# Causal attention in a two-layer trunk: the mask moves from 64 TensorE products into a custom VectorE operation, and the first scores from double to single PSUM banks

## The chip, the cores and the metric

The kernel runs on one core of a Trainium2 chip. The metric is the device time of one execution in microseconds (us); less is better. The time before is the median of three runs.

## The reference, cut to what matters

All of it is float32, with a batch of 1, a sequence of 1024 and a model width of 1024. There are two layers: an mLSTM mixer with an MLP, then causal latent attention (8 heads) with an MLP. The change touches the causal softmax of the second layer:

```python
def block(args):                     # 128 queries of all heads
    qn_b, qr_b, start = args
    s = (jnp.einsum('bqhd,bkhd->bhqk', qn_b, k_nope)
         + jnp.einsum('bqhd,bkd->bhqk', qr_b, k_rope)).astype(jnp.float32) * scale
    qpos = start + jnp.arange(B_QBLOCK, dtype=jnp.int32)
    s = jnp.where(kpos[None, :] <= qpos[:, None], s, -jnp.inf)
    p = jax.nn.softmax(s, axis=-1)
    return jnp.einsum('bhqk,bkhd->bqhd', p.astype(v.dtype), v)
```

Around it, each layer computes `x + g1 * rmsnorm(mixer(modulate(rmsnorm(x))))` and then `x + g2 * rmsnorm(mlp(modulate(rmsnorm(x))))`, and the modulation (`ada`) comes from products of a condition vector with wide weight matrices.

## The kernel before, in words

Products of float32 tensors are made of three products of parts: each factor is split into a high and a low part, and `mm3` (L255, L256, L257) adds low x high, high x low and high x high in one PSUM bank. Weights come by DMA into `raw`, a ring of four 128x1024 buffers in SBUF; ScalarE copies out the high part (L190, L549) and VectorE subtracts it for the low part (L191, L550). The rows of probabilities, `pr`, lie in the same ring.

PSUM has eight banks of 128 x 512 floats: `ps` and `pc` are rings of two single banks, `pm` is a ring of two double banks. The dense stream of the MLPs accumulates in `pm` and `ps`; VectorE takes the sums out of `pm` at L199. `pc` serves transposes and small projections.

`two_streams` weaves two generators: the dense stream of an MLP, and the other one, which has the attention. The sequence is done in two halves of 512 queries. While the attention of the first half runs (955 to 1210 us), the dense stream is layer 0's MLP for the second half; while that of the second half runs (1565 to 1825 us), it is the MLP of layer 1 for the first. A scheduler then orders each engine's queue from its own estimates of how long instructions take; a kernel's queues are worked off in that order.

The attention works in units: one head and a pair of blocks of 128 queries, j = 0 and 1 in the first half, j = 2 and 3 in the second. The two blocks of a unit, e = 0 and 1, see n = (2j + e + 1) x 128 keys. A unit goes like this:

- `score_mm` makes the scores of one block, per group of up to 512 keys (at least 256 columns wide): four products at L1584 to L1587, for the group that holds the diagonal the mask product at L1589, and the last product at L1590. The mask product adds `maskA` (0 on and below the diagonal, -1e30 above) to 128 columns, with the bf16 identity `identb`. There are 64 of them. L1586 and L1587 need T, the turned rope part of the queries, which VectorE finishes at L1570.
- For j = 0 and 1 both blocks of a unit share one `pm` (a bank for each); for j = 2 and 3 each block has its own `pm`.
- `softmax` takes the negative maximum of the row (L1594, VectorE), scales it (L1595), makes the exponential of the scores with that as bias and with their sum (L1596, ScalarE, from PSUM into `pr`), inverts the sum (L1597) and normalises the row (L1598). POOL clears the 128 columns behind the shorter block's row (L1600).
- `attend` turns the probabilities by transposes into `pc` (L1704), splits them, and multiplies them with the values in `ps`.

At the start of the kernel SyncE's queue loads x, the first weights of the first projection (L1926) and the modulation weights of the first part (L376, L341); TensorE sums the modulation up (L344, L356), and the first dense products (L255) wait for the modulated x. The mask constants are built there too, on POOL and VectorE.

Of the kernel before, what the change touches and what calls it, by code (L numbers as in the profile page):

```python
# [11 lines left out]
BF16 = mybir.dt.bfloat16  # L12
I32 = mybir.dt.int32
AF = mybir.ActivationFunctionType
ALU = mybir.AluOpType
AX = mybir.AxisListType

P = 128
D = 1024
S = 1024  # L20
H = 512
# [62 lines left out]
def kernel(  # L84
# [27 lines left out]
    nc = tc.nc  # L112
# [4 lines left out]
    ts = lambda i, n: slice(i * n, (i + 1) * n)  # L117
# [18 lines left out]
    def tmp(dt=F32):  # L136
        return sb.tile([P, 512], dt, tag="tmp", bufs=TMP, name=f"tmp_{next(uid)}")

    def tmc(dt=F32):
        return sb.tile([P, 512], dt, tag="tmc", bufs=TMC, name=f"tmc_{next(uid)}")  # L140
# [10 lines left out]
    def pc():  # L151
        return pp.tile([P, 512], F32, tag="pc", bufs=2, name=f"pc_{next(uid)}")

    def pm():
        return pp.tile([P, 2, 512], F32, tag="pm", bufs=2, name=f"pm_{next(uid)}")

    def const(shape, dt, name):
        return sb.tile(shape, dt, tag=name, bufs=1, name=name)
# [102 lines left out]
    ident = const([P, P], F32, "ident")  # L261
# [186 lines left out]
    def gate(i, g, s):  # L448
        nc.vector.tensor_mul(mods[:, i], g, s)
        return mods[:, i]  # L450

    identb = const([P, P], BF16, "identb")
    nc.vector.tensor_copy(identb, ident)
    maskA = const([P, P], BF16, "maskA")
    mt = tmp()
    nc.gpsimd.memset(mt[:, :P], 0.0)
    nc.gpsimd.affine_select(
        out=mt[:, :P], in_=mt[:, :P], pattern=[[-1, P]], compare_op=ALU.is_ge,
        fill=-1e30, base=0, channel_multiplier=1,
    )  # L460
    nc.vector.tensor_copy(maskA, mt[:, :P])

    e8 = const([P, NH], F32R, "e8")
    nc.vector.memset(e8.bitcast(F32), 0.0)
# [15 lines left out]
    Cst = const([P, 4, VE], F32, "Cst")  # L480
# [39 lines left out]
    def sums_rstd(acc, n, y):  # L520
        pt = pc()
        nc.tensor.matmul(pt, ones, acc, start=True, stop=True)
        v, t = tmc(), acc
        nc.vector.tensor_scalar(v, pt, 1.0 / n, EPS, ALU.mult, ALU.add)
        rsqrt_(y, v, t)
        return y
# [838 lines left out]
    def rope_perm():  # L1365
        for q in range(4):
            nc.vector.tensor_copy(perm[:, ts(q, 32)], ident[:, ts(q ^ 1, 32)])
# [50 lines left out]
    def latent(hf, behind):  # L1418

        ready = []

        def load(b):
            with tc.high_priority(PRIO):
                w = []
                for i in range(2):
                    t = raw(F32R)
                    if i == 0:
                        t = sb.tile([P, 1024], F32R, tag="ws", bufs=WS, name=f"lw_{next(uid)}")  # L1430
                    nc.sync.dma_start(t.bitcast(F32), lw[b, i])
                    w.append(t.rearrange("p (a b) -> p a b", b=P))
                ready.append(w)

        load(0)
        load(1)
        yield 0
        h = hf.xn

        def proj(b):  # L1440
            if b < 4:
                load(b + 2)
            w, pt = ready.pop(0), pc() if b == 2 else ps()
            for k in range(KD):
                mm3(pt, w[0][:, k], w[1][:, k], h.hi[k], h.lo[k], k == 0, k == KD - 1)
            return pt

        lb = lambda b: lbias[:, b : b + 1]
        hf.cs = hdv()
        for i in range(2):  # L1450
            nc.sync.dma_start(hf.cs[:, i], rope_d[i][:, ts(hf.i, H)])
        if hf.i:
            hf.kk = [hd(F32R), hd(F32R)]
            for i in range(2):
                nc.sync.dma_start(hf.kk[i][:, 0:H].bitcast(F32), kkd[i])
        else:
            t = hdv(F32R)
            hf.kk = [t[:, 0], t[:, 1]]
        s = ts(hf.i, H)
        ck, cq0, cq1 = k4v(), k4v(), k4v()  # L1460
        cq = [cq0[:, 0], cq0[:, 1], cq1[:, 0]]
        def scaled(o, m):

            pt = proj(m)

            if not rx:
                rx.append(sums_rstd(hf.xx, D, Cst.rearrange("p a b -> p (a b)")[:, :H]))
            nc.vector.tensor_mul(o, pt, rx[0])
            return o

        def based(o, m):
            nc.scalar.activation(o, scaled(o, m), AF.Identity, bias=lb(m))

        rx = []
        for m in range(2):
            based(ck[:, m], m)
        rp = rope(scaled(tmc(), 2), hf, lb(2))
        next(rp)
        yield 0
        rs = rstd_steps([ck[:, 0], ck[:, 1]], 256)  # L1480
        next(rs)
        based(cq[0], 3)
        yield 0
        kr = last_of(rp)
        rstd_k = last_of(rs)
        nc.scalar.copy(hf.kk[0][:, s], kr)
        nc.vector.tensor_sub(hf.kk[1][:, s], kr, hf.kk[0][:, s].bitcast(F32))
        if not hf.i:
            for i in range(2):
                nc.sync.dma_start(kkd[i], hf.kk[i].bitcast(F32))  # L1490
        for m in range(1, 3):
            based(cq[m], 3 + m)
        yield 0
        behind()
        rs = rstd_steps(cq, 384)
        next(rs)
        hi, lo = k4v(F32R), k4v(F32R)
        with paced():
            for m in range(2):
                u = ck[:, m]  # L1500
                nc.vector.scalar_tensor_tensor(u, u, col(KVL + m, 1), rstd_k, ALU.mult, ALU.mult)
                split_mod(hi[:, m], lo[:, m], u, None)
        hf.ckv = ([hi[:, m] for m in range(2)], [lo[:, m] for m in range(2)])
        yield 3 - hf.i
        rstd = last_of(rs)
        yield 0
        ah, al, b = k4v(F32R), k4v(F32R), k4v(F32R)
        his, los = [ah[:, 0], ah[:, 1], b[:, 0]], [al[:, 0], al[:, 1], b[:, 1]]
        for m in range(3):
            u = cq[m]  # L1510
            nc.vector.scalar_tensor_tensor(u, u, col(QL + m, 1), rstd, ALU.mult, ALU.mult)
            split_mod(his[m], los[m], u, None)
        hf.cq = (his, los)
        yield 1

    SCALE = float((128 + 64) ** -0.5)
# [56 lines left out]
    def score_mm(o2, kk, q, kn, i):  # L1573

        qn, T = q
        qs = ts(i % 4, P)
        n = (i + 1) * P
        qh, ql, qT = qn[:, 0, qs], qn[:, 1, qs], T[:, qs]
        for g in range((n + 511) // 512):
            w = max(256, min(512, n - g * 512))  # L1580
            o = o2(g)
            ks = slice(g * 512, g * 512 + w)
            kh, kl = kn[0][:, ks], kn[1][:, ks]
            nc.tensor.matmul(o[:, :w], ql, kh, start=True, stop=False)  # L1584
            nc.tensor.matmul(o[:, :w], qh, kl, start=False, stop=False)
            nc.tensor.matmul(o[:, :w], qT, kk[1][:, ks], start=False, stop=False)  # L1586
            nc.tensor.matmul(o[:, :w], qT, kk[0][:, ks], start=False, stop=False)  # L1587
            if g == i // 4:
                nc.tensor.matmul(o[:, ts(i % 4, P)], identb, maskA, start=False, stop=False)  # L1589
            nc.tensor.matmul(o[:, :w], qh, kh, start=False, stop=True)  # L1590

    def softmax(f, pr, n, even):
        m, l = small(1), small(1)
        nc.vector.reduce_max(m, f, axis=AX.X, negate=True)  # L1594
        nc.vector.tensor_scalar(m, m, SCALE, None, ALU.mult)  # L1595
        nc.scalar.activation(pr[:, :n], f, AF.Exp, bias=m, scale=SCALE, accum_out=l)  # L1596
        nc.vector.reciprocal(l, l)  # L1597
        nc.vector.tensor_scalar(pr[:, :n], pr[:, :n], l, None, ALU.mult)  # L1598
        if even:
            nc.gpsimd.memset(pr[:, n : n + P], 0.0)  # L1600

    def scores(kk, unit):

        (_, q, kn, _), j = unit
        prs = []
        if j < 2:
            st = pm()
            pr = raw().rearrange("p (a b) -> p a b", b=512)
            for e in range(2):
                score_mm(lambda g: st[:, e], kk, q, kn, 2 * j + e)  # L1610
            for e in range(2):
                n = (2 * j + e + 1) * P
                softmax(st[:, e, :n], pr[:, e], n, e == 0)
                prs.append(pr[:, e])
        else:
            for e in range(2):
                st = pm()
                n = (2 * j + e + 1) * P
                score_mm(lambda g: st[:, g], kk, q, kn, 2 * j + e)
                pr = raw()  # L1620
                softmax(st.rearrange("p a b -> p (a b)")[:, :n], pr, n, e == 0)
                prs.append(pr)
        return prs
# [549 lines left out]
    drain(p1)  # L2173
    two_streams(with_weight_sums(f0), behind(bg_latent(), 4))
    rope_perm()


    B = {}
# [91 lines left out]
    fill = all_out()  # L2270
    v = None
    dense = mlp(1, hfs[1], u1, [4] * 8, True, B)
    n = 0
# [34 lines left out]
```

## Time and profile before

| | |
|---|---|
| median of 3 runs | 2361.49 us (2361.12 to 2361.56) |
| the profiled execution | 2359.22 us |
| its span | 2357.3 us |
| mean granted TensorE clock | 0.997 |
| TensorE, VectorE, ScalarE, POOL busy | 98%, 68%, 47%, 7% |
| first attention, 955 to 1210 us: TensorE, VectorE busy | 250.9, 194.7 us |
| second attention, 1565 to 1825 us: TensorE, VectorE busy | 255.2, 159.1 us |

A group's row gives line, engine, operation, output <- inputs, shape and count, then busy us and mean ns, then the idle time before it and what ended that. In a timeline the columns are start and duration in us, and a bracket holds the idle time ahead of the instruction and its releaser. Matmuls are pipelined: each is listed with its whole passage, so several overlap, and the room that one takes is read from start to start. PEld is the loading of weights for them.

### The profile page before, as it was taken

How to read it: one execution, taken by the hardware profiler on the slowest of the kernel's cores; microseconds unless marked ns; L12 is line 12 of the kernel's file. 1: busy time of each engine (PE TensorE's matmuls, PEld its weight loads, DVE VectorE, ACT ScalarE, POOL GpSimd, SP SyncE). 2: the span in 40 equal slices, each digit the busy share in tenths (PEclk: the TensorE clock that was granted, in tenths of full speed). 3: DMA queues.
4: the chain of work that ended last, by engine and by line, in shares of the span. 5: the costliest groups of instructions: out<-in, count | busy, mean ns of one | idle time of the engine just before them, and what ended most of it. 6: DMA issues, size and time to landing. Idle time of an engine off the chain costs nothing.

```text
span 2357.3 us, 32527 instructions
## 1 busy us (share of the span) xinstructions
PE 2321.8 (98%) x12181; PEld 1959.9 (83%) x12181; DVE 1605.7 (68%) x2657; ACT 1098.2 (47%) x1826; POOL 155.0 (7%) x353
## 2 busy tenths in 40 slices
PE   7999999999999999999999999999999999999998
PEld 5888898888888888888888888888888888989997
DVE  6677876867685777777764967765656488557556
ACT  4355335654343354334444554434444445655543
POOL 1010000000001110111010110010001000000000
PEclk9999999999999999999999999999999999999999
DMA  9452664545566876667764665885544553656562
GB/s 314 144 153 82 191 184 149 156 141 163 174 184 179 284 222 188 184 195 207 211 160 126 199 200 183 274 274 172 163 134 134 143 164 97 185 173 217 166 185 88
DMA packets 408349, 420.76 MB, mean 178 GB/s; under 512 B 27427, under 2 KB 310112, under 8 KB 404608
## 3 DMA queue, kind: packets, MB, share of 16 engines
q1 hardware_dynamic: 402272, 385.02, 52.1%
q0 software_dynamic: 5920, 33.66, 6.5%
q8 instruction: 96, 1.57, 0.3%
q14 instruction: 61, 0.50, 0.1%
HBM read 359.37 MB, written 92.80 MB: 192 GB/s over the span
## 4 chain that ended last, share of the span: by engine, by line
PE 89%; DVE 5%; DMA 4%; ACT 1%; issue 1%; SPq 0%; DVEq 0%; ACTq 0%
PE ps L255 15%; PE ps L257 15%; PE ps L256 15%; PE pm L255 10%; PE pm L256 10%; PE pm L257 10%; DMA raw<-in_mlp_w_dram 2%; PE pc L256 2%; PE pc L257 2%; PE pc L255 2%; PE pc L1704 1%; DMA raw<-in_a_w_in_dram 1%; PE pm L1590 1%; PE pm L899 1%; PE pm L1584 1%
## 5 line engine op out<-in xcount | busy, mean ns | idle before, releaser
L255 PE MATMUL ps<-k,wl 128*128 128x512 f32 (+1 forms) x1432 | 546.3, 381 | 1.6 <-DVE wl L191 1.3
L257 PE MATMUL ps<-k,wh 128*128 128x512 f32 (+1 forms) x1432 | 539.0, 376 | 0.0
L256 PE MATMUL ps<-k,wh 128*128 128x512 f32 (+1 forms) x1432 | 537.4, 375 | 0.0
L549 ACT CAST wh<-raw 128x1024 fp32r<-128x1024 f32 x272 | 285.0, 1051 | 481.4 <-PE ps L255 149.0
L550 DVE TENSOR_TENSOR wl<-raw,wh 128x1024 fp32r<-128x1024 f32 x272 | 331.7, 1221 | 249.4 <-ACT wh L549 155.4
L255 PEld LDWEIGHTS ps<-k,wl 128*128 128x128 f32 x1432 | 269.6, 188 | 53.7 <-issue 3.6
L257 PEld LDWEIGHTS ps<-k,wh 128*128 128x128 f32 x1432 | 269.4, 188 | 50.1 <-issue 0.7
L256 PEld LDWEIGHTS ps<-k,wh 128*128 128x128 f32 x1432 | 269.8, 188 | 48.9 <-issue 1.7
L199 DVE TENSOR_TENSOR k<-k,pm 128x512 f32<-128x512 f32 (+1 forms) x254 | 210.9, 858 | 83.3 <-PE pm L257 82.0
L191 DVE TENSOR_TENSOR wl<-raw,wh 128x1024 fp32r<-128x1024 f32 (+2 forms) x110 | 128.1, 1166 | 115.6 <-ACT wh L190 115.4
L255 PE MATMUL pm<-hd,wl 128*128 128x512 f32 x512 | 201.4, 393 | 0.5 <-ACT hd L531 0.5
L256 PE MATMUL pm<-hd,wh 128*128 128x512 f32 x512 | 199.3, 390 | 0.2 <-DVE hd L532 0.2
L257 PE MATMUL pm<-hd,wh 128*128 128x512 f32 x512 | 199.3, 390 | 0.0
L255 PE MATMUL pm<-wh,hd 128*128 128x512 f32 x488 | 192.2, 394 | 2.9 <-ACT raw L1596 2.5
L256 PE MATMUL pm<-wl,hd 128*128 128x512 f32 x488 | 190.3, 390 | 0.0
L257 PE MATMUL pm<-wh,hd 128*128 128x512 f32 x488 | 190.2, 390 | 0.0
L190 ACT CAST wh<-raw 128x1024 fp32r<-128x1024 f32 (+2 forms) x110 | 109.4, 996 | 172.3 <-PE ps L255 82.9
L1596 ACT ACTIVATE raw<-pm,sm 128x128 f32<-128x128 f32 (+3 forms) x64 | 47.5, 742 | 152.4 <-DVE sm L1595 122.8
L532 DVE TENSOR_TENSOR hd<-tmp,hd 128x512 fp32r<-128x512 f32 x128 | 88.0, 688 | 38.6 <-ACT hd L531 37.9
L255 PEld LDWEIGHTS pm<-hd,wl 128*128 128x128 f32 x512 | 96.2, 188 | 21.0 <-ACT hd L531 0.9
L256 PEld LDWEIGHTS pm<-hd,wh 128*128 128x128 f32 x512 | 96.2, 188 | 20.5 <-DVE hd L532 0.5
L257 PEld LDWEIGHTS pm<-hd,wh 128*128 128x128 f32 x512 | 96.1, 188 | 20.1
(391 smaller groups left out, 4274.9 us busy)
## 6 DMA issues: line engine op xcount, KB each, us to landing
raw<-in_mlp_w_dram SPq DMA_DIRECT2D x240, 512.0 KB, 4.3
raw<-in_ada_w_dram SPq DMA_DIRECT2D x80, 512.0 KB, 4.6
raw<-in_a_w_in_dram SPq DMA_DIRECT2D x48, 512.0 KB, 4.4
sums<-in_mlp_w_dram POOLq DMA_DIRECT2D x96, 256.0 KB, 4.5
raw<-sums SPq DMA_DIRECT2D x64, 256.0 KB, 3.7
xs<-k SPq DMA_DIRECT2D x40, 256.0 KB, 5.6
raw<-in_kv_ada_w_dram SPq DMA_DIRECT2D x16, 512.0 KB, 4.1
raw<-in_a_w_out_dram SPq DMA_DIRECT2D x16, 512.0 KB, 4.9
```

Of the source, the lines that this page charges most:

```text
L190: nc.scalar.copy(hi[:, :n], r[:, :n])
L191: i = nc.vector.tensor_sub(lo[:, :n], r[:, :n], hi[:, :n].bitcast(F32))
L199: return f(*a, **k)
L255: nc.tensor.matmul(o, ll, rh, start=start, stop=False, **m)
L256: nc.tensor.matmul(o, lh, rl, start=False, stop=False, **m)
L257: pe_last[0] = nc.tensor.matmul(o, lh, rh, start=False, stop=stop, **m)
L532: nc.vector.tensor_sub(lo, u, hi.bitcast(F32))
L549: nc.scalar.copy(hi, u)
L550: nc.vector.tensor_sub(lo, u, hi.bitcast(F32))
L899: nc.tensor.matmul(nv[:, r, i], hf.PT[p_][:, r, cs], v[2 * p_ + r], start=g == 0, stop=True,)
L1584: nc.tensor.matmul(o[:, :w], ql, kh, start=True, stop=False)
L1596: nc.scalar.activation(pr[:, :n], f, AF.Exp, bias=m, scale=SCALE, accum_out=l)
```

## The change

It has three parts, and one that follows from them.

1. The mask products and their constants are removed. `maskw`, a bf16 row of 1024 columns whose last 128 hold the triangle and whose others are 0, takes their place; POOL makes it after `rope_perm`, in the space of `Cst`, a state of the mLSTM that is done by then. What lay there (`rx`, a row of factors) goes to a free half of `cq1`.
2. `softmax` calls `tensor_tensor_reduce`, a custom VectorE operation: `pr = (scores + maskw) * -SCALE`, and m = the minimum of that row (started from 3e38). It is given `maskw[:, 1024 - n:]`, so that the triangle falls on the diagonal block. The exponential then reads `pr` in place, from SBUF, with scale -1 and bias m. VectorE's separate scaling of m is gone.
3. For j = 0 the unit's two blocks share one single bank of `pc`, 256 columns each.

```diff
-    identb = const([P, P], BF16, "identb")
-    nc.vector.tensor_copy(identb, ident)
-    maskA = const([P, P], BF16, "maskA")
-    mt = tmp()
-    nc.gpsimd.memset(mt[:, :P], 0.0)
-    nc.gpsimd.affine_select(
-        out=mt[:, :P], in_=mt[:, :P], pattern=[[-1, P]], compare_op=ALU.is_ge,
-        fill=-1e30, base=0, channel_multiplier=1,
-    )
-    nc.vector.tensor_copy(maskA, mt[:, :P])
...
-                rx.append(sums_rstd(hf.xx, D, Cst.rearrange("p a b -> p (a b)")[:, :H]))
+                rx.append(sums_rstd(hf.xx, D, cq1[:, 1]))
...
-            if g == i // 4:
-                nc.tensor.matmul(o[:, ts(i % 4, P)], identb, maskA, start=False, stop=False)
             nc.tensor.matmul(o[:, :w], qh, kh, start=False, stop=True)
...
-        nc.vector.reduce_max(m, f, axis=AX.X, negate=True)
-        nc.vector.tensor_scalar(m, m, SCALE, None, ALU.mult)
-        nc.scalar.activation(pr[:, :n], f, AF.Exp, bias=m, scale=SCALE, accum_out=l)
+        nc.vector.tensor_tensor_reduce(
+            pr[:, :n], f, maskw[:, 1024 - n :], -SCALE, 3e38, ALU.add, ALU.min, m
+        )
+        nc.scalar.activation(pr[:, :n], pr[:, :n], AF.Exp, bias=m, scale=-1.0, accum_out=l)
...
-            st = pm()
+            st = pm() if j else pc().rearrange("p (a b) -> p a b", b=256)
...
     rope_perm()
+    maskw = Cst.rearrange("p a b -> p (a b)")[:, :H].bitcast(BF16)
+    nc.gpsimd.memset(maskw, 0.0)
+    nc.gpsimd.affine_select(
+        out=maskw[:, 896:], in_=maskw[:, 896:], pattern=[[-1, P]], compare_op=ALU.is_ge,
+        fill=-1e30, base=0, channel_multiplier=1,
+    )
```

The line numbers shift: L1584 to L1587 become L1573 to L1576, L1590 becomes L1577, the new operation is L1581, the exponential L1584, the reciprocal L1585, the normalising L1586, POOL's clearing L1588, the transposes L1692.

What follows from it is a new order of the queues. On TensorE the first scores of the first pair of heads (j = 0) are these before; `pm_8564` holds head 0, `k_1448_8320` is its queries' high part:

```order
4316 L257 MATMUL pm_8541<-hd_8158,wh_8348 128x512
4317 L1584 MATMUL pm_8564<-k_1448_8320,k_1469_8440 128x256
4318 L1585 MATMUL pm_8564<-k_1448_8320,k_1469_8440 128x256
4319 L1586 MATMUL pm_8564<-hd_7841,k_1475_8472 128x256
4320 L1587 MATMUL pm_8564<-hd_7841,k_1475_8472 128x256
4321 L1589 LDWEIGHTS identb
4322 L1589 MATMUL pm_8564<-maskA,identb 128x128
4323 L1590 MATMUL pm_8564<-k_1448_8320,k_1469_8440 128x256
4324 L1584 MATMUL pm_8564<-k_1448_8320,k_1469_8440 128x256
```

At the same place after, `pc_8559` holds head 0 and `pc_8584` head 1:

```order
4316 L257 MATMUL pm_8536<-hd_8153,wh_8343 128x512
4317 L1573 MATMUL pc_8559<-k_1447_8315,k_1468_8435 128x256
4318 L1574 MATMUL pc_8559<-k_1447_8315,k_1468_8435 128x256
4319 L1573 MATMUL pc_8584<-k_1448_8316,k_1470_8448 128x256
4320 L1574 MATMUL pc_8584<-k_1448_8316,k_1470_8448 128x256
4321 L1575 MATMUL pc_8559<-hd_7836,k_1474_8467 128x256
4322 L1576 MATMUL pc_8559<-hd_7836,k_1474_8467 128x256
4323 L1577 MATMUL pc_8559<-k_1447_8315,k_1468_8435 128x256
4324 L1573 MATMUL pc_8559<-k_1447_8315,k_1468_8435 128x256
```

The mask's two rows are gone, and the two products of head 1 that don't need T stand ahead of those of head 0 that do. The rest of TensorE's order is nearly the same.

On VectorE the softmax of these units is, before (`sm` are the 128x1 values):

```order
1134 L199 TENSOR_TENSOR k_1255_7413<-k_1255_7413,pm_9267 128x1024
1135 L1594 TENSOR_REDUCE sm_9304<-pm_9290 128x1
1136 L1595 TENSOR_SCALAR sm_9304<-sm_9304 128x1
1137 L1597 RECIPROCAL sm_9305<-sm_9305 128x1
1138 L1594 TENSOR_REDUCE sm_9312<-pm_9290 128x1
1139 L1598 TENSOR_SCALAR raw_9291<-raw_9291,sm_9305 128x128
1140 L1595 TENSOR_SCALAR sm_9312<-sm_9312 128x1
```

and after:

```order
1133 L199 TENSOR_TENSOR k_1254_7408<-k_1254_7408,pm_9246 128x1024
1134 L1581 ISA raw_9270,sm_9281<-pc_9269,Cst 128x128
1135 L1581 ISA sm_9281 128x1
1136 L1581 ISA raw_9270,sm_9288<-pc_9269,Cst 128x256
1137 L1581 ISA sm_9288 128x1
1138 L1585 RECIPROCAL sm_9282<-sm_9282 128x1
1139 L1581 ISA raw_9295,sm_9306<-pc_9294,Cst 128x128
```

Each of the new operations is a main instruction with the write of its accumulator right behind it, and the reciprocal, which needs the exponential, stands behind two of them.

On SyncE's queue the loads behind x are, before:

```order
5 L317 DMA k_8_102<-in_x_dram 128x1024
6 L1926 DMA raw_282<-in_a_w_in_dram 128x4x256
7 L376 DMA k_33_234<-in_ada_w_dram 128x2x512
8 L341 DMA k_35_239<-in_ada_w_dram 128x2x512
9 L376 DMA k_36_243<-in_ada_w_dram 128x2x512
```

and after, where the first weight load stands behind all eight modulation loads:

```order
5 L317 DMA k_8_102<-in_x_dram 128x1024
6 L376 DMA k_32_225<-in_ada_w_dram 128x2x512
7 L341 DMA k_34_230<-in_ada_w_dram 128x2x512
8 L376 DMA k_35_234<-in_ada_w_dram 128x2x512
9 L341 DMA k_36_238<-in_ada_w_dram 128x2x512
10 L376 DMA k_37_242<-in_ada_w_dram 128x2x512
11 L341 DMA k_38_246<-in_ada_w_dram 128x2x512
12 L376 DMA k_39_250<-in_ada_w_dram 128x2x512
13 L341 DMA k_40_254<-in_ada_w_dram 128x2x512
14 L1914 DMA raw_273<-in_a_w_in_dram 128x4x256
```

The split of that load on VectorE (L191) moves from ahead of the modulation of x to behind it.

## The prediction

> **What bounds the kernel now.** I read the page first, then the waits of TensorE, then the timeline around the lines that the change touches. Three lines of the page say which engine sets the time: TensorE is busy 98% of the span, and the chain that ended last runs on it for 89%.
>
> ```profile
> span 2357.3 us, 32527 instructions
> PE 2321.8 (98%) x12181; PEld 1959.9 (83%) x12181; DVE 1605.7 (68%) x2657; ACT 1098.2 (47%) x1826; POOL 155.0 (7%) x353
> PE 89%; DVE 5%; DMA 4%; ACT 1%; issue 1%; SPq 0%; DVEq 0%; ACTq 0%
> ```
>
> So a product that leaves TensorE's stream shortens the run by the room it took, and VectorE's work counts only where TensorE stands and waits for it. The waits of TensorE (total, times, longest, in us) hold four rows that the change can reach:
>
> ```profile
> PE pm L1584 <- DVE k L199: 2.9, 4, 0.9
> PE pm L255 <- ACT raw L1596: 2.5, 4, 1.1
> PE pm L1584 <- DVE sm L1046: 1.2, 3, 0.5
> PE pc L1704 <- DVE raw L1598: 0.5, 3, 0.2
> ```
>
> The first and third are the first products of scores (j = 0) waiting for a double bank. The second is the dense stream waiting for a double bank that an exponential still reads. The fourth is transposes waiting for normalised rows.
>
> **The change part by part.** *The mask products.* There are 64, each with its weight load:
>
> ```profile
> L1589 PE MATMUL pm<-maskA,identb x64: 229/229/231, 961.3 to 1812.7; 128*128 128x128 bf16 x64
> ```
>
> The 229 ns is latency in a pipeline, so I price a mask product from start to start. Here two score groups stand next to each other in the timeline, a 512-wide one without mask (two of its products) and a 256-wide one with it:
>
> ```profile
> 1568.73 0.40 PE L1587 MATMUL pm<-hd,k 128*128 128x512 f32 x1
> 1568.97 0.39 PE L1590 MATMUL pm<-k,k 128*128 128x512 f32 x1
> 1569.19 0.28 PE L1584 MATMUL pm<-k,k 128*128 128x256 f32 x1
> ...
> 1569.55 0.28 PE L1587 MATMUL pm<-hd,k 128*128 128x256 f32 x1
> 1569.67 0.23 PE L1589 MATMUL pm<-maskA,identb 128*128 128x128 bf16 x1
> 1569.71 0.37 PE L1590 MATMUL pm<-k,k 128*128 128x256 f32 x1
> 1569.91 0.39 PE L1584 MATMUL pm<-k,k 128*128 128x512 f32 x1
> ```
>
> A 256-wide product normally takes 0.12 (L1587's, 1569.55 to 1569.67). From L1587 to the next group's start are 1569.91 - 1569.55 = 0.36, where two products would take 0.24: the mask costs 0.12, or 0.13 with the digits that rounding hides. I take 0.131 for all widths: 64 x 0.131 = 8.4 us. Nothing covers it, since TensorE is the bound. It goes: **-8.4**.
>
> *Single banks for j = 0.* In the first attention each pair of heads begins like this on TensorE (pair 0), with VectorE's last step of the rope in pair 1 below it:
>
> ```profile
> 960.01 0.39 PE L257 MATMUL pm<-hd,wh 128*128 128x512 f32 x1
> 960.75 0.39 PE L1584 MATMUL pm<-k,k 128*128 128x256 f32 x1 [0.35 <-DVE sm L1046]
> 962.07 0.36 PE L1590 MATMUL pm<-k,k 128*128 128x256 f32 x1
> 963.15 0.38 PE L1584 MATMUL pm<-k,k 128*128 128x256 f32 x1 [0.71 <-DVE k L199]
> 1031.14 0.69 DVE L1570 TENSOR_TENSOR k<-tmc,tmp 64x512 fp32r<-64x512 f32 x1
> 1033.74 0.39 PE L1584 MATMUL pm<-k,k 128*128 128x256 f32 x1 [0.45 <-DVE sm L1046]
> ```
>
> A 512-wide product takes about 0.22 (1568.97 to 1569.19 above), so 960.01 to 960.75 lost 0.51, which the row calls 0.35. After the mask product a 256-wide one takes 0.20 (1569.71 to 1569.91), so 962.07 to 963.15 lost 0.88, called 0.71. Seven waits with 2.9 + 1.2 = 4.1 in the view, and some 0.16 more each, make 5.2 us. With `pc` these products no longer wait for the dense stream's accumulators. What is late next? The rope's result ends at 1031.83, 1.9 before the products that need it, so it takes nothing back. A `pc` bank is also held, but its last readers run several us earlier. I count all of it: **-5.2**; the ends are 0 and -5.2.
>
> *The double bank is given back earlier.* Before, `pm` came free behind the exponential; now it comes free behind VectorE's operation.
>
> ```profile
> 1606.39 0.95 DVE L1594 TENSOR_REDUCE sm<-pm 128x1 f32<-128x768 f32 x1
> 1607.64 0.90 ACT L1596 ACTIVATE raw<-pm,sm 128x768 f32<-128x768 f32 x1 [2.19 <-PE pm L257]
> 1608.68 0.50 PE L255 MATMUL pm<-wh,hd 128*128 128x512 f32 x1 [1.13 <-ACT raw L1596]
> ```
>
> VectorE is done at 1607.34 and the bank is free at 1608.54: it would come 1.2 earlier, more than the 1.13 waited. Four such waits hold 2.5, with 0.16 each 3.1: **-3.1**, ends 0 and -4.
>
> *The new operation.* On VectorE's queue it is two instructions, a main one and a 128x1 write of the accumulator, in the place of the reduction and the 128x1 scaling. No row of before has it. Its neighbours (by line and form; count, total, mean ns) are:
>
> ```profile
> L1594 DVE TENSOR_REDUCE sm<-pm 128x1 f32<-128x1024 f32 x8 | 9.8, 1223 | 3.4 <-PE pm L1590 3.4
> L1594 DVE TENSOR_REDUCE sm<-pm 128x1 f32<-128x512 f32 x8 | 5.4, 672 | 0.0
> L1468 DVE TENSOR_TENSOR k<-ps,Cst 128x512 f32<-128x512 f32 x10 | 6.7, 687 | 4.2 <-PE ps L257 3.9
> L383 DVE SCALAR_TENSOR_TENSOR tma<-raw,cond,tma 128x512 f32<-128x512 f32 x126 | 95.1, 755 | 13.4 <-DMA raw<-in_kv_ada_w_dram 6.9 <-DMA raw<-in_ada_w_dram 5.0
> L789 DVE TENSOR_TENSOR_SCAN tmc<-ones,mcol,tmc 8x128 f32<-8x128 f32 x8 | 3.8, 470 | 0.2
> L1595 DVE TENSOR_SCALAR sm<-sm 128x1 f32<-128x1 f32 x64 | 9.7, 151 | 1.0
> L1198 ACT ACTIVATE tmp<-tmp 128x512 f32<-128x512 f32 x96 | 60.7, 632 | 2.5
> L1197 ACT ACTIVATE tmp<-ps 128x512 f32<-128x512 f32 x96 | 56.8, 592 | 68.6 <-PE ps L257 68.5
> L1596 ACT ACTIVATION_READ_ACCUMULATOR raw<-pm,sm 128x1 f32 x64 | 12.3, 193 | 0.0
> ```
>
> The reduction costs (1223 - 672) / 512 = 1.08 ns an element. An addition of a PSUM and an SBUF tensor (687 at 512) is 15 ns dearer, a three-input one (755) 83 ns. The scan takes 470 at 128; with the 151 of a tiny operation taken off, 2.5 ns an element, since each element waits for the one before. The new operation also carries a running minimum, but off the path of its output. It is nearest to the addition, so I take the reduction's time plus 15. The accumulator's write lies between nothing and ScalarE's 193; I take L1595's own 151. ScalarE reading SBUF is 632 - 592 = 40 ns slower. So the chain of one softmax grows by 0.015 + 0.04, about 0.05 us, ends -0.10 (no separate write) and +0.17 (755-like and 193). It touches TensorE where transposes wait for L1598, in each head's j = 3 unit at most: 8 x 0.05 = **+0.4**, ends -0.8 and +1.4.
>
> The operation now needs its `raw` buffer itself, for which the exponential waited before. VectorE would stand still with L199 and L550 behind it. Such a buffer is seen to be free when POOL clears its tail; for the second head's 896 columns, and for the reduction that the new operation replaces, that stands so in the timeline:
>
> ```profile
> 1585.00 0.20 POOL L1600 MEMSET raw<- 128x128 f32 x1 [1.19 <-PE pc L1704]
> 1588.39 1.08 DVE L1594 TENSOR_REDUCE sm<-pm 128x1 f32<-128x896 f32 x1
> ```
>
> It was free 3.4 before the reduction, so I count nothing; where it is late, VectorE loses what ScalarE lost before.
>
> *The start.* Without the constants the scheduler puts the first weight load behind eight loads of modulation weights on SyncE's queue, and its split on VectorE behind the modulation. Around the first products (29.78) the timeline says this, with a later split, and below it a window (busy us of PE, PEld, DVE, ACT, POOL; granted clock, DMA share, GB/s):
>
> ```profile
> 24.03 1.03 PE L356 MATMUL pc<-ones,tmp 128*128 128x1 f32 x8
> 27.93 1.92 PE L344 MATMUL pc<-hd,tma 128*32 128x512 f32 x4 [2.87 <-DVE tmc L381]
> 29.78 0.80 PE L255 MATMUL pm<-k,wl 128*128 128x512 f32 x1
> 33.71 1.22 DVE L191 TENSOR_TENSOR wl<-raw,wh 128x1024 fp32r<-128x1024 f32 x1
> 26.40:33.10 6.70, 5.17 (x13) 2.41 (x15) 6.67 (x12) 3.50 (x5) 0.00 (x0) 0.50 1.05 387
> ```
>
> The queue is full (DMA share 1.05, 387 GB/s), so one load of 128 x 1024 x 4 bytes less ahead brings the modulation 0.524 MB / 387 GB/s = 1.35 us forward, and the first products, which start 5.7 behind L356, with it. A split of 1.22 that is no longer done early takes up to that back, and so do the loads that follow and land no earlier. I take **-1.0**, ends -1.5 and +2. In these 6.7 us the granted clock was 0.50. The Trainium skill ("TensorE: Matmul & The Clock Gate", the clock gate's states) puts the half clock down to an idle window of about 3.4 us. The trace agrees in so far as TensorE stood still for 2.9 ahead of L344 at 27.93. By that rule a longer pause could cost a second such window; the +2 is from rows: nine 512-wide products at twice their 0.22.
>
> Sum: -8.4 - 5.2 - 3.1 + 0.4 - 1.0 = -17.3 us. The profiled execution took 2359.2 (span 2357.3); -17.3 gives 2341.9. The runs' median 2361.5 lies 2.3 above it, so I forecast **2344**. The ends add up to -5 and -20, the mask products whole in both, or 2357 and 2342.
>
> **The rivals.** *Only the mask products go.* TensorE's other waits come back as waits for something else: `pc`, the rope, the next double bank. For it speaks that each wait on the list has an engine with a full queue behind it; against it, that rope and bank were ready 1 to 2 us earlier in the rows above. Then -8.4, up to 3 more or less: about 2353.
>
> *The operation is slow.* Each operation with an output and a running result could take two passes' time per element. On the other side of before it needs this: the two units of a head's j = 3 (896 and 1024 elements) stand one behind the other on VectorE, and TensorE waits for the second. At twice the slope a head loses 1920 x 1.08 = 2.1 us, eight heads 16.6, and the banks come free no earlier (the 3.1 is lost), so -17.3 + 16.6 + 3.1 = +2.4, or 2364. At the scan's 2.5 ns a head loses 1920 x 1.42 = 2.7, eight heads 21.8: +7.6, or 2369, **slower**. It turns into a loss from about twice the slope. For it speaks the scan's row; against it, that a minimum is a reduction like L1594, whose row is at full rate. The Trainium skill ("Vector Engine (DVE) Microarchitecture Reference", points that are easy to get wrong) says that one family of two-input operations with an accumulator runs at half rate when both inputs are non-bf16 in SBUF. Here one input is in PSUM and the mask is bf16, so by its letter it does not apply; no row of before tests it.
>
> *More than the sum.* VectorE's order in pair 0 has no reciprocal between two reductions any more, so it waits less for ScalarE; the softmax of later units could start earlier and other stalls of 0.2 to 0.3 at transposes go: 3 to 6 us more, about 2339.
>
> **How the numbers follow.** The forecast has 0.62, only the mask products 0.20, more than the sum 0.09, the slow operation 0.09 (half of it at 2364, a third at 2369, the rest between). 0.2% is 4.7 us, about what a measurement of this kernel can tell from no change: same is 2356.8 to 2366.2. Faster by more takes the first three, 0.91, less 0.01 for the edge of the second: 0.90. Same 0.06, slower 0.04. The range reaches from 2338 (more than the sum) to 2355 (most of only the mask products); the likeliest case alone has 2341 to 2351.
>
> **What would show it.** The profile after should have no L1589; L1577 starting one product behind L1576; no wait of the j = 0 scores for L199; no dense product waiting for the exponential; the main instruction of L1581 near 1.24 us at 1024 and 0.70 at 512; first dense products at about 28.8. I am wrong if L1581 takes over 1.6 us at 1024, if TensorE's waits in the two attentions stay near the 7 us of now under other names, or if the first products start later than 30.

## The result, and the profile after

The changed kernel takes 2343.51 us, the median of four runs (2343.07 to 2347.77), against 2361.52 before: 18.0 us less, a ratio of 0.9926 with the 95% interval [0.9914, 0.9938]. The forecast was 2344. The profiled execution is the one of 2347.77, the longest of the four; what it has beyond the others is shown below, and a second profile of the same kernel (e12, span 2341.8) stands beside it.

The page's lines on the span, the engines and the chain that ended last:

```profile
span 2346.1 us, 32377 instructions
PE 2315.4 (99%) x12117; PEld 1962.0 (84%) x12117; DVE 1598.8 (68%) x2655; ACT 1100.7 (47%) x1826; POOL 157.4 (7%) x353
PE 92%; DVE 3%; DMA 3%; issue 1%; ACT 1%; SPq 0%; DVEq 0%; ACTq 0%
```

TensorE has 64 matmuls less (12117 for 12181) and its share of the chain rose from 89% to 92%, VectorE's fell from 5% to 3%. The four rows of TensorE's waits that the prediction quoted are gone from the view; none of those pairs of waiter and releaser stands there any more. What the list has in and near the places of the change is this (total, times, longest):

```profile
PE pm L255 <- ACT k L523: 4.4, 1, 4.4
PE pm L1575 <- DMA k<-td: 1.7, 1, 1.7
PE ps L256 <- DVE hd L521: 1.2, 2, 0.9
```

The first is the start of the kernel, the second the first scores of the second attention, which wait for a load (1.1 before), the third the split of turned probabilities in the first (no wait for it stands in that part of the view before). A whole 256-wide score group of a diagonal block now looks like this on TensorE (timeline of e12, the same kernel):

```profile
1563.57 0.28 PE L1573 MATMUL pm<-k,k 128*128 128x256 f32 x1
1563.69 0.28 PE L1574 MATMUL pm<-k,k 128*128 128x256 f32 x1
1563.81 0.28 PE L1575 MATMUL pm<-hd,k 128*128 128x256 f32 x1
1563.93 0.29 PE L1576 MATMUL pm<-hd,k 128*128 128x256 f32 x1
1564.05 0.28 PE L1577 MATMUL pm<-k,k 128*128 128x256 f32 x1
1564.17 0.40 PE L1573 MATMUL pm<-k,k 128*128 128x512 f32 x1
```

Five products, each 0.12 behind the one before. The new operation, its accumulator's write and the exponential behind them have these rows (count, total, mean ns):

```profile
L1581 DVE CUSTOM_DVE_ANT_0 raw<-pm,Cst 128x1024 f32<-128x1024 f32 x8 | 9.8, 1224 | 4.2 <-PE pm L1577 4.2
L1581 DVE CUSTOM_DVE_ANT_0 raw<-pm,Cst 128x512 f32<-128x512 f32 x8 | 5.4, 677 | 0.0
L1581 DVE DVE_READ_ACCUMULATOR2_ANT sm<- 128x1 f32 x64 | 5.2, 82 | 0.0
L1584 ACT ACTIVATE raw<-raw,sm 128x1024 f32<-128x1024 f32 x8 | 9.2, 1154 | 16.0 <-DVE sm L1581 8.3 <-DVE sm L1035 7.8
```

The operation costs what the reduction did (1224 for 1223 at 1024, 677 for 672 at 512) though it also reads a mask and writes a row. The write takes 82 ns where the scaling took 151, and the exponential is 34 ns slower from SBUF. More than these durations, it is the gaps that changed. Before, for head 0's 1024 columns:

```profile
1590.29 1.22 DVE L1594 TENSOR_REDUCE sm<-pm 128x1 f32<-128x1024 f32 x1 [0.62 <-PE pm L1590]
1591.43 0.15 DVE L1597 RECIPROCAL sm<-sm 128x1 f32<-128x1 f32 x1
1591.55 0.15 DVE L1595 TENSOR_SCALAR sm<-sm 128x1 f32<-128x1 f32 x1
1591.79 1.12 ACT L1596 ACTIVATE raw<-pm,sm 128x1024 f32<-128x1024 f32 x1 [0.91 <-DVE sm L1595]
```

And after, the same unit:

```profile
1588.40 1.22 DVE L1581 CUSTOM_DVE_ANT_0 raw<-pm,Cst 128x1024 f32<-128x1024 f32 x1 [0.55 <-PE pm L1577]
1589.55 0.08 DVE L1581 DVE_READ_ACCUMULATOR2_ANT sm<- 128x1 f32 x1
1589.55 0.16 DVE L1585 RECIPROCAL sm<-sm 128x1 f32<-128x1 f32 x1
1589.67 1.15 ACT L1584 ACTIVATE raw<-raw,sm 128x1024 f32<-128x1024 f32 x1 [0.65 <-DVE sm L1581]
```

From the start of the maximum to the start of the exponential it took 1.50, now 1.27. The scaling had to wait for the reduction's result and another operation (here a reciprocal) ran between the two; the accumulator's write starts 0.07 before the listed end of its main instruction, and in VectorE's order nothing stands between. This unit is one of the short ones. Over all 64 rows, the time from the end of the maximum to the start of the exponential was 0.46 in the mean before (0.28 to 1.21), since other work, such as operations of 0.74 at L383, stood between, in the units of 384 and 512 columns above all; it is 0.07 after (0.04 to 0.10).

What the profiled execution has beyond the others stands in its windows (busy us of PE, PEld, DVE, ACT, POOL; granted clock, DMA share, GB/s), and in the same ten microseconds of e12:

```profile
264.00:274.00 10.00, 8.34 (x39) 6.23 (x38) 7.77 (x9) 5.58 (x12) 2.03 (x1) 0.83 0.88 274
1566.00:1570.00 4.00, 4.00 (x16) 3.38 (x15) 0.83 (x2) 0.92 (x2) 0.00 (x0) 0.58 1.02 421
```

```profile
264.00:274.00 10.00, 8.71 (x48) 6.72 (x46) 8.78 (x11) 5.70 (x12) 2.04 (x1) 1.00 0.87 265
```

Narrower windows of the profiled execution hold just the stretches at half clock:

```profile
268.88:272.29 3.41, 3.41 (x10) 2.62 (x9) 3.41 (x5) 2.07 (x3) 2.03 (x1) 0.50 0.79 252
1565.95:1569.36 3.41, 3.41 (x13) 2.83 (x12) 0.83 (x2) 0.56 (x1) 0.00 (x0) 0.50 1.02 420
```

TensorE waits at the first place for a weight split (L191), and at the second for a load (L1575); so it does in e12. Behind these waits, of 1.7 us each in this execution, its clock was halved for 3.4 us, which by that costs 1.7 each time (a half-clock stretch below); in e12 the same waits were 1.3 and 0.5 and the clock stayed at 1.00.

### The profile page after: what moved, and what is told of

Same layout as the page of the kernel before. It is cut to its first block, busy times and chain, and to the rows that moved or that the text cites. A ratio compares the mean times of both kernels' runs of the same rounds, so it can differ in the third digit from the quotient of the medians.

```text
span 2346.1 us, 32377 instructions
## 1 busy us (share of the span) xinstructions
PE 2315.4 (99%) x12117; PEld 1962.0 (84%) x12117; DVE 1598.8 (68%) x2655; ACT 1100.7 (47%) x1826; POOL 157.4 (7%) x353
## 4 chain that ended last, share of the span: by engine, by line
PE 92%; DVE 3%; DMA 3%; issue 1%; ACT 1%; SPq 0%; DVEq 0%; ACTq 0%
PE ps L255 16%; PE ps L256 15%; PE ps L257 15%; PE pm L256 10%; PE pm L255 10%; PE pm L257 10%; PE pc L255 2%; PE pc L257 2%; PE pc L256 2%; PE pc L1692 1%; DMA raw<-in_a_w_in_dram 1%; PE pm L888 1%; PE pm L1575 1%; PE pm L1576 1%; PE pm L1577 1%
## 5 line engine op out<-in xcount | busy, mean ns | idle before, releaser
L199 DVE TENSOR_TENSOR k<-k,pm 128x512 f32<-128x512 f32 (+1 forms) x254 | 210.7, 858 | 83.4 <-PE pm L257 82.2
L191 DVE TENSOR_TENSOR wl<-raw,wh 128x1024 fp32r<-128x1024 f32 (+2 forms) x110 | 128.0, 1166 | 117.4 <-ACT wh L190 117.3
L1036 POOL COPY sm<-sm 128x1 f32<-128x1 f32 x128 | 49.0, 392 | 945.8 <-DVE sm L1035 942.3
```

The costliest lines, as they stand in the source:

```text
L191: i = nc.vector.tensor_sub(lo[:, :n], r[:, :n], hi[:, :n].bitcast(F32))
L199: return f(*a, **k)
L1036: now = nc.gpsimd.tensor_copy(seen, flag)
```

## The experiments

Each was timed in five or more runs beside the kernel before on the same chip (2361.26 for e1 to e4, 2359.64 for e5 to e8, 2360.23 for e9 to e12). The differences to it:

| run | mask products | operation | j = 0 banks | median | to before | ratio, interval | first attention | second attention |
|---|---|---|---|---|---|---|---|---|
| e5 | kept | old | single | 2356.14 | -3.5 | 0.9986 [0.9977, 0.9995] | 308.3 | 301.4 |
| e6 | kept | new | double | 2354.32 | -5.3 | 0.9974 [0.9965, 0.9983] | 313.5 | 289.3 |
| e3 | gone | old | double | 2356.67 | -4.6 | 0.9981 [0.9972, 0.9990] | 313.2 | 291.6 |
| e2 | kept | new | single | 2351.06 | -10.2 | 0.9958 [0.9944, 0.9973] | 307.4 | 290.3 |
| e4 | gone | old | single | 2350.21 | -11.1 | 0.9954 [0.9942, 0.9967] | 303.9 | 292.5 |
| e7 | gone | new | double | 2349.35 | -10.3 | 0.9951 [0.9938, 0.9963] | 309.9 | 284.4 |
| e1 | gone, constants made | new | single | 2342.97 | -18.3 | 0.9923 [0.9911, 0.9936] | 306.1 | 285.6 |
| e12 | gone (after again) | new | single | 2343.53 | -16.7 | 0.9929 [0.9917, 0.9942] | 305.7 | 284.3 |

The last two columns are lengths of stretches in one profiled execution of each: the time between the same two dense products by count, those that stand at 926 and 1239 us before (around the first attention), and at 1540 and 1835 (around the second). Before has 313.0 and 294.8. After has 305.5 and 287.8; its second stretch has 3.4 us at half clock in it, that of e5 twice as much.

Each part alone brings 3.5 to 5.3, together 13.4; all three bring 16.7 to 18.3 (for e12, which is after itself, 17 to 19 were expected). By the medians a part is worth more as the last one added than alone, but a difference here is uncertain by 2 to 3 us. The stretches bear that out for the mask products (3.1 in both together from before to e3, 6.0 from e2 to e1) and not for the banks (4.7 in the first from before to e5, 4.3 from e7 to e12).

**The start and the mask products (e1, e2).** e1 is after with the constants back (an excerpt):

```diff
+    identb = const([P, P], BF16, "identb")
...
+    nc.vector.tensor_copy(maskA, mt[:, :P])
```

e2 is e1 with the products back too:

```diff
+            if g == i // 4:
+                nc.tensor.matmul(o[:, ts(i % 4, P)], identb, maskA, start=False, stop=False)
```

> The kernel after, with the mask constants of before still made (and unused), which puts the start of SyncE's and VectorE's queues back to the order of before. If the new order at the start gains the 1.0 us forecast, this takes 2344.5 against the 2343.5 of after. If the start is worth nothing, as the after profile suggests (first high x high product at 30.64 against 30.80), it takes 2343 to 2344. If the new order costs through the half clock, it is faster than after by up to 2.

> The kernel after, with the constants and the 64 mask products put back (the mask is then added twice). Only the products differ from e1. Sum theory: e1 plus 8.4, so about 2352. Rival (products hide in the waits that TensorE has anyway): e1 plus 0 to 3. Rival (all of the gain is the products, banks and operation bring nothing): 2361.

e1 gave 2342.97, as after: the new order at the start is worth nothing that these times can measure. After's own profile shows why.

```profile
20.16 1.05 PE L344 MATMUL pc<-k,tma 128*32 128x512 f32 x4 [0.62 <-DMA k<-in_ada_w_dram]
27.47 0.80 PE L255 MATMUL pm<-k,wl 128*128 128x512 f32 x1 [4.39 <-ACT k L523]
28.20 1.92 PE L344 MATMUL pc<-hd,tma 128*32 128x512 f32 x4
30.05 0.79 PE L256 MATMUL pm<-k,wh 128*128 128x512 f32 x1
```

Against before, the modulation is summed 2.0 earlier (20.16 for 22.14) and the first product starts 2.3 earlier (27.47 for 29.78), but the next modulation's products (L344), which stood ahead of it before, now stand behind it, and the second product comes at 30.05, where before had it at 30.37. The 109th dense product, past the start, begins at 60.18 before, at 60.30 after and 60.25 in e12, and at 59.24 in e1: nothing is gained there.

e2 took 8.1 more than e1, with nothing but the products between them in the code: 126 ns each, where the prediction's start-to-start reading said 131. That agreement is closer than the runs can bear. Between the two profiled executions the attention stretches differ by 6.0, 1.3 in the first and 4.7 in the second. The rest lies ahead of both: e2 is 1.0 later at the 109th dense product, and it loses 1.6 around 268 us in a half-clock stretch (0.83 over 264 to 274) that e1's execution had not.

**Mask products and banks without the operation (e3, e4).** Both leave the causal mask out of the computation. e3 is before without constants and products; e4 takes the single banks in addition.

```diff
-            if g == i // 4:
-                nc.tensor.matmul(o[:, ts(i % 4, P)], identb, maskA, start=False, stop=False)
```

> The kernel before, without mask products and constants and with nothing in their place: the causal mask is left out of the computation. Sum theory: 2361.5 - 8.4 - 0 for the start = 2353, and the waits of the scores for L199 and of the dense stream for the exponential stay in the profile. Rival (freed room turns into longer waits for banks, since VectorE sets the pace): 2357 or more.

> As e3 (no causal mask), with the scores of j = 0 in single banks. Sum theory: e3 minus 5.2, 2348, and the waits for L199 are gone. Rival (a wait for something else takes their place): e3 minus 0 to 2.

e3 gained 4.6, about half of the 8.4, and e4 another 6.5. TensorE's waits in e3 from 940 to 1215 us begin with:

```profile
PE pm L1573 <- DVE k L199: 4.4, 4, 1.1
PE pm L1573 <- DVE sm L1035: 0.8, 1, 0.8
```

That is 5.2 where before had 4.1 under the same two names, and new waits of 0.9 follow it in the view. Around the first attention e3's profile is 0.2 us longer than before's: the 32 products that left there, 4.2 by the prediction's price, saved nothing. The longer waits account for about 2.0 of that, 1.1 of it at scores that still had to wait for a double bank; the rest, in an order of the queues that differs too, is not explained. Nor does a double bank always take back what is removed ahead of it: e7 has no mask products and e6 has them, both with double banks and with the same two waits (4.1 and 3.9 in the view), and there e7 is 3.6 shorter. With single banks (e4) the same stretch took 9.1 less than before, which is the products' half (4.2) and about what the waits had (5.2). In the second attention, from 1540 to 1835 us, e4 still waits for the exponential:

```profile
PE pm L255 <- ACT raw L1583: 3.5, 6, 1.1
PE pc L1691 <- DVE raw L1585: 0.8, 4, 0.2
```

**One part alone, and one part less (e5, e6, e7).** e5 is before with one line changed, and e7 is after with it changed back; e6 is e2 with double banks.

```diff
-            st = pm()
+            st = pm() if j else pc().rearrange("p (a b) -> p a b", b=256)
```

> The kernel before, with the scores of j = 0 in single banks and nothing else changed. Sum theory: 2361.5 - 5.2 = 2356.3. Rival (the wait comes back under another name): 2360 to 2362.

> The kernel after, with mask products and constants put back and the scores of j = 0 in double banks: of the change only the new operation is left (the mask is added twice). Sum theory: 2361.5 - 3.1 + 0.4 = 2358.8, and no dense product waits for the exponential. Rival (the waits in the second attention are set by the whole softmax, not by the bank): 2361 to 2362.

> The kernel after with the scores of j = 0 in double banks again. Sum theory: 2343.5 + 5.2 = 2348.7, with 4 us of waits for L199 in the profile. Rival (the order that VectorE's operation gives already removes those waits): 2344 to 2345.

e5 gained 3.5 where 5.2 were expected. In the first attention, where the banks were changed, its profile gained 4.7; that execution is the longest of its twelve (2363.31), with three half-clock stretches, and its second attention, where the dense products waited 5.0 for the exponential (2.5 before), says little. e7 lost 6 to 8 against after (2349.35; 7.7 by the differences to before, 6.4 against e12) where 5.2 were. The waits for L199 are back in e7, from 940 to 1215 us:

```profile
PE pm L1573 <- DVE k L199: 3.7, 4, 1.1
PE pm L1573 <- DVE sm L1035: 0.4, 2, 0.3
```

e6 gained 5.3, twice what the sum had for the operation (2.7), and all of it in the second attention (5.5). There its view has one row left, and neither the exponential nor the normalising is in it:

```profile
PE pm L1586 <- DMA k<-td: 1.4, 1, 1.4
```

**A slower operation (e8).** The operation is issued twice in a row.

```diff
-        nc.vector.tensor_tensor_reduce(
+        for _ in range(2):
+            nc.vector.tensor_tensor_reduce(
```

> The kernel after with the new operation issued twice in a row, so that it takes 2.6 us instead of 1.3 at 1024 columns and VectorE works 46 us more in all. The rival of the slow operation priced twice the slope at 8 x 2.1 us and the lost 3.1: here, with the accumulator's write twice too, 2343.5 + 8 x 2.5 + 3.1 = 2366, slower than before. If only the last unit of each head lies on TensorE's path, 8 x 1.3 = 10: 2354. If VectorE has room for it, 2344 to 2347.

It took 2367.22, 7.6 more than before (ratio 1.0031 [1.0019, 1.0043]), and about 25 more than after, by the differences to before, where the expectation had about 23. So the rival of a slow operation was priced about right: had it taken twice as long, the change would have brought no gain. Two of its rows, the operation's and TensorE's largest wait in the second attention:

```profile
L1582 DVE CUSTOM_DVE_ANT_0 raw<-pm,Cst 128x1024 f32<-128x1024 f32 x16 | 19.5, 1219 | 1.4 <-PE pm L1577 1.3
PE pc L1693 <- DVE raw L1587: 14.7, 9, 2.5
```

The transposes wait nine times for a normalised row, 14.7 us in all. VectorE is busy 69% of the run, 44 us more than after (1643.0 for 1598.8), and more than half of that shows in the time. It does so in one place: against e12 the first attention is 1.6 longer and the second 26.3, of which about 5 are three half-clock stretches of this profiled execution, the longest of its five.

**Why the operation gains twice its price (e9, e10).** The prediction had the double bank come free earlier. e9 is e2 with the exponential reading PSUM as before, so that a bank is held until it is done:

```diff
-        nc.scalar.activation(pr[:, :n], pr[:, :n], AF.Exp, bias=m, scale=-1.0, accum_out=l)
+        nc.scalar.activation(pr[:, :n], f, AF.Exp, bias=m, scale=SCALE, accum_out=l)
```

e10 is after with a 128x1 operation put where the scaling stood:

```diff
+        nc.vector.tensor_scalar(m, m, 1.0, None, ALU.mult)
         nc.scalar.activation(pr[:, :n], pr[:, :n], AF.Exp, bias=m, scale=-1.0, accum_out=l)
```

> The kernel of e2 (new operation, single banks, mask products kept), but the exponential reads the scores from PSUM with the old scale, as before, so that a bank is held until the exponential is done; the operation still writes its row, which the exponential overwrites. Theory that the operation's gain is the earlier bank: e2 (10.2 below before) plus about 4, the four or more waits of the dense stream for the exponential are back, the transposes' waits stay away. Rival (the gain is the shorter chain from the maximum to the exponential): e2 plus 0 to 0.5.

> The kernel after with one more 128x1 operation on VectorE (times 1.0) between the new operation and the exponential, as L1595 stood there before: the chain from scores to probabilities gets 0.25 us longer again and nothing else. Theory of the shorter chain: the waits of the transposes for the normalised row come back, six of 0.3, so 1.5 to 2 more than after, and 0.5 to 1.5 more where the scheduler again puts other work between the two. Rival (those waits went for another reason): 0 to 0.5 more than after.

e9 took 10.2 less than before, the same as e2. The theory of the earlier bank falls: with the bank held as long as before, no dense product waited for the exponential in the view, since the exponential itself comes sooner:

```profile
1588.20 1.23 DVE L1594 CUSTOM_DVE_ANT_0 raw<-pm,Cst 128x1024 f32<-128x1024 f32 x1 [0.80 <-PE pm L1590]
1589.47 1.12 ACT L1597 ACTIVATE raw<-pm,sm 128x1024 f32<-128x1024 f32 x1 [0.93 <-DVE sm L1594]
```

It starts 1.27 behind the maximum's start, as in after. What the prediction's 2.7 lacked can be read from the starts of TensorE's products in the second attention. Before, the dense products lose 4.3 us in seven waits for the exponential, not 3.1 in four, and the transposes 1.8 in six waits for normalised rows, which the sum had not counted as a gain; e6 has 0.3 of the two left, and its second attention is 5.5 shorter.

e10 took 5.0 more than e12, more than either theory gave. Its profiled execution is the longest of its five (2351.51), with half-clock stretches near 268 and 1569 us that e12's has not. Its waits, the first two from 940 to 1215 us and the third from 1540 to 1835:

```profile
PE ps L256 <- DVE hd L521: 1.8, 3, 1.0
PE ps L255 <- ACT hd L520: 1.5, 2, 1.1
PE pc L1693 <- DVE raw L1587: 0.6, 3, 0.2
```

The transposes' waits are back (three in the view, six of about 0.3 read from start to start, as before). The dense products' waits are not: the bank is released early here. So either an early bank (e10) or a short chain (e9) removes those; the waits of the transposes need the short chain. The rest of the 5 us is new in the first attention, which is 3.0 longer than in e12. There the products with the values wait for probabilities that are split later, and in e10's order VectorE has other operations between maximum and scaling again. The same unit of 384 columns in e12 and in e10:

```profile
980.91 0.55 DVE L1581 CUSTOM_DVE_ANT_0 raw<-pm,Cst 128x384 f32<-128x384 f32 x1
981.50 0.62 ACT L1584 ACTIVATE raw<-raw,sm 128x384 f32<-128x384 f32 x1 [5.84 <-DVE sm L1581]
```

```profile
980.86 0.55 DVE L1581 CUSTOM_DVE_ANT_0 raw<-pm,Cst 128x384 f32<-128x384 f32 x1
981.42 0.75 DVE L383 SCALAR_TENSOR_TENSOR tma<-raw,cond,tma 128x512 f32<-128x512 f32 x1
982.08 0.15 DVE L1584 TENSOR_SCALAR sm<-sm 128x1 f32<-128x1 f32 x1
982.31 0.62 ACT L1585 ACTIVATE raw<-raw,sm 128x384 f32<-128x384 f32 x1 [7.04 <-issue]
```

Over the 64 rows of e10, the time from the end of the maximum to the start of the exponential is 0.47 in the mean again (0.23 to 1.57), as before. That this order, and not the 0.15 us of the operation itself, makes those 3 us is likely by this, but no run parts the two.

**A load that is late (e11).** After with the first head of the second attention loaded ahead of the last pair's preparation:

```diff
+                first = loaded_head(0)
                 yield from pairs[p_]
...
-                h_ = loaded_head(hh)
+                h_ = loaded_head(hh) if hh else first
```

> The kernel after with the first head's keys, queries and values of the second attention loaded ahead of the last pair's preparation, not behind its stores. After, the first scores there wait 0.6 for the scheduler's earlier start and 1.8 for a load (L1575), and in its profiled execution TensorE then ran 3.4 us at half clock. If these loads are what is late: 2 to 4 faster than after, with no such wait. Rival (the loads hold the queue and the buffers back for the last pair): the same or slower, with new waits at 1530 to 1560.

> The kernel after itself, beside the others on the same chip: 17 to 19 below before.

e11 took 2342.39 (0.9928 [0.9915, 0.9940]), 1.1 less than e12, where 2 to 4 less than after were expected; the intervals overlap, so it is not shown to be faster. In its profile TensorE's view has no wait from 1540 to 1835 us; after's had the load at L1575, 1.7, with 0.4 ahead of it at L1573, and e12's 0.5 at L1575. The stretch around the second attention is as long as e12's to 0.2 us.

## Why the prediction was right, point by point

The time was right to half a microsecond, which is luck: its terms were not all right, their errors cancel, and the runs tell differences only to 2 or 3 us. That the products leave TensorE's stream, that the waits for banks and for the exponential go, and that the operation is not slow came true.

- **Mask products, -8.4.** With the other parts in place the size is 8.1 by the times and 6.0 by the stretches (e2 against e1). The prediction said that nothing covers them since TensorE is the bound. That failed for this part by itself: alone it brings 4.6 (e3), and nothing in the first attention, where waits for VectorE and ScalarE became longer. These waits are about half of what is missing there; the other half is open.
- **Single banks, -5.2.** The mechanism was right: the waits for L199 go with the single banks and are back without them (e7). But all of it was counted, and a smaller wait took their place, products with the values for split probabilities (1.2 in the view after, 1.3 in e12). The size was 3.5 alone (e5), 6.5 behind the removal of the products (e4 against e3), and 6 to 8 as the last part (e7); in the first attention alone these are 4.7, 9.3 and 4.3.
- **Earlier bank, -3.1, and the new operation, +0.4.** This step failed in its cause. The operation's time was right (1224 and 677 ns; 1238 and 687 were expected), but the chain behind it was said to grow by 0.05 and became 0.23 shorter up to the exponential in the unit shown, 0.39 in the mean of all: the work that stood between was not in the sum. It is worth 5.3 alone, and 7.2 as the last part (e1 against e4), where the sum had 2.7: the waits for the exponential held 4.3 and not 3.1, and the transposes' 1.8, which go too, were not in it. e9 shows that the earlier bank was not needed for it.
- **The start, -1.0.** It was nothing: what came earlier was given back by the modulation products that moved behind the first product, and the 109th dense product begins no earlier than before (60.25 to 60.30 for 60.18). The time of e1 alone could not tell 1.0 from nothing.
- **The rivals.** "Only the mask products go" was wrong as a result (2353): the other waits went, and what came in their place is smaller. The slow operation did not come, by the durations; its price for twice the slope was 2.4 more than before, and e8, with the operation issued twice, took 7.6 more, in part at half clock. "More than the sum" rightly named the stalls at the transposes that would go, but not the time.
- **The rule on half rate.** The Trainium skill ("Vector Engine (DVE) Microarchitecture Reference", points that are easy to get wrong) says that one family of two-input operations has half the throughput when both sources are non-bf16 in SBUF. With one source in PSUM and a bf16 mask, which the rule does not speak of, the trace shows the time of the plain reduction (1224 for 1223 ns at 1024 columns); whether the operation is of that family, and two such sources, were not tried.

## What to carry to other kernels

Work taken off the bound engine can be worth less than its price where that engine waits soon after: look for the next wait on its queue, and whether what ends it moves too. What a part is worth depends on the others that are in place: around the first attention, mask products and banks together bring 9.1 with the old operation (e4), where each alone brings -0.2 and 4.7, but with the new one 7.4 (e6 to e1), where each alone brings 3.6 (e7) and 6.1 (e2). Each build also gets a new order of its queues, so one such difference is no law. A tiny operation between a reduction and its user on another engine can cost more than its 0.15 us, since it is a place where the scheduler puts other work: put back, it cost 5.0 us here (e10).

## What the runs showed of the hardware

- A custom VectorE operation with two inputs, an output and a running minimum takes the time of a plain reduction (1224 for 1223 ns at 1024 columns), and its accumulator's write 82 ns, which starts before the main instruction's listed end.
- TensorE's clock was halved for 3.4 us behind waits of 1.7 us in one execution (0.50 from 268.88 to 272.29 and from 1565.95 to 1569.36), and stayed at 1.00 behind one of 1.3 in another of the same kernel (e12). In e10 the same wait of 1.3 was followed by such a stretch (0.83 from 264 to 274), so its length alone does not decide. The Trainium skill ("TensorE: Matmul & The Clock Gate", the clock gate's states) speaks of an idle window of about 3.4 us; in these rows half of that or less was enough, in some executions.
